# One layer of a hybrid S5 and attention trunk: second keys behind the output projection, memory scaled at eviction, and the first up pair by seven block products

## The chip, the core and the metric

The kernel runs on one core of one Trainium2 chip, as one launch that computes a whole layer in float32. TensorE (PE) multiplies, VectorE (DVE), ScalarE (ACT) and GpSimd (POOL) work on tiles, SyncE (SP) issues most of the loads, POOL most of the stores. The metric is the device time of an execution in microseconds: the median of 3 runs was 1415.62 us (1415.24 to 1419.94).

## The reference

The batch is 1, with 1024 rows of 1024 channels, 256 memory rows, 4 cross-attention heads of 256 and a feed-forward width of 2816.

```python
def memory_cross_attention(h, mem_n, wq, wkv, wo):
    q = (h @ wq).reshape(bsz, seq, XA_HEADS, XA_HEAD_DIM)
    kv = mem_n @ wkv
    k = kv[..., :D_MODEL].reshape(bsz, m, XA_HEADS, XA_HEAD_DIM)
    v = kv[..., D_MODEL:].reshape(bsz, m, XA_HEADS, XA_HEAD_DIM)
    s = jnp.einsum('bqhd,bmhd->bhqm', q, k).astype(jnp.float32) / math.sqrt(XA_HEAD_DIM)
    p = jax.nn.softmax(s, axis=-1)
    o = jnp.einsum('bhqm,bmhd->bqhd', p.astype(v.dtype), v).reshape(bsz, seq, D_MODEL)
    return o @ wo

def swiglu(h, w_gate, w_up, w_down):
    return (jax.nn.silu(h @ w_gate) * (h @ w_up)) @ w_down

def reference(...):
    mem_n = rms_norm(mem, mem_g)
    h = rms_norm(x, mix_pre_g)
    proj = h @ w_in
    ...
    y_ssm = s5_mixer(...)
    y_fox = forgetting_attention(q, k, v, f_logit).reshape(bsz, seq, FOX_WIDTH)
    y_mix = jnp.concatenate([rms_norm(y_ssm, ssm_out_g), rms_norm(y_fox, fox_out_g)], axis=-1)
    x = x + rms_norm(y_mix @ w_out, mix_post_g)
    h = rms_norm(x, xa_pre_g)
    x = x + rms_norm(memory_cross_attention(h, mem_n, xa_wq, xa_wkv, xa_wo), xa_post_g)
    h = rms_norm(x, ffn_pre_g)
    x = x + rms_norm(swiglu(h, w_gate, w_up, w_down), ffn_post_g)
```

## The kernel before

Products in float32 are made of three matmuls: both operands are split into a high part, made by ACT (L113), and a low part, made by DVE as the difference (L115, or L117 with a gain), and `mm3` (L122 to L124) adds high by high, high by low and low by high. In the traces a split thus shows as an ACTIVATE at L113 followed by a TENSOR_TENSOR at L115 on the same tile. Weights are loaded by SP into `raw` (two buffers) and split into `whl` (three buffers) by `load_w`.

The stages are these. The input projection, the S5 scan and the FoX attention take the first 490 us. The attention (L732 scores, L739 and L741 the exponentials, L760 transposes, L774 values) is a chain through all engines, so other work is woven into it as fillers: the gate of the S5 branch, its rows (L838), the load and scaling of the memory (L962 on), the 16 tiles of memory keys and values (`mem_tile`, L969) and the first half of the keys (`build_a(0)`). `mem_load` multiplies the transposed memory by the reciprocal root of each memory row, broadcast over the partitions (`rb`, made by `row_bcast`), with 8 multiplications by DVE at L965; then it splits each piece. Each memory tile is evicted from PSUM by ACT (L977) and stored to `kv_d` by POOL.

The output projection follows (490 to 540 us): per row tile n, in the order 3, 4, 5, 6, 7, 0, 1, 2, the S5 part of the sum is loaded from DRAM (L1068, named `a<-t_d` or `b<-t_d` in the profile after the view that it is read through), a row tile of x is fetched (L1071), PE multiplies, DVE evicts with the addition (L1078), ACT squares (L1080), POOL multiplies by a gain (L1082), the reciprocal root follows (L137 to L145), DVE adds to x (L1086) and POOL stores (L1090). Woven in are the first value weights: value tiles are loaded into `t`, split, and multiplied with the split output weights (`g<-whl,t`, L122 to L124).

`build_a(1)` makes the other half of the keys: for two heads it loads a key tile from `kv_d` (L1006), splits it (L1007) and multiplies it with the query weights. The tiles come from the buffers "b" and "a", which the output projection uses too.

Cross-attention runs to about 770 us. The feed-forward part works on 11 pairs of tiles of 256 hidden channels. From the second pair on a product by a pair is made by the seven block products of Strassen and Winograd's scheme (`gate_up`), with operands S1 to S4 of sums and differences of weight blocks, made by POOL at L1405 and split. The first pair uses plain products, 8 block products for the gate and 8 for the up projection (`plain_product`), each of 12 matmuls of 128x512 at L1302. hB holds the activations' blocks and their sums T1 to T4. The down projection ends the kernel, from 1198 us.

The order of instructions on each engine is set by the framework's scheduler, from priorities, from `tc.issue_after` (an instruction is put behind another) and from when buffers come free. It is fixed when the kernel is built; each engine then executes its list in that order, and one that waits holds everything behind it. Buffers are counted pools: 3 of "t2", 2 of "yt", 2 each of "a" and "b", 1 of "e".

Of the kernel before, what the change touches and what calls it, by code (L numbers as in the profile page):

```python
# [52 lines left out]
def layer(ctx: ExitStack, tc: tile.TileContext, a, out):  # L53
# [113 lines left out]
        return v[:, 0], v[:, 1]  # L167

    def row_bcast(r, n):
        rb = t2t([P, n * P]) if n == 2 else tt("d", [P, n * P])  # L170
        ps = (s_ps if n > 4 else g_ps)([P, n * P])
        for j in range(n):
            pe.transpose(ps[:, j * P:(j + 1) * P], r[:, j:j + 1].broadcast_to([P, P]), ident)
        for j in range(0, n, 4):
            cs = slice(j * P, min(j + 4, n) * P)
            act.activation(out=rb[:, cs], in_=ps[:, cs], func=AF.Copy)
        return rb
# [778 lines left out]
    def mem_load(r, out):  # L956
        rb = row_bcast(r, 2)
        yield
        mh, ml = slab([P, KT, 256]), slab([P, KT, 256])
        for k in range(0, KT, 4):  # L960
            m = raw([P, 4, 256])
            sp.dma_start(out=m, in_=a["memT"].rearrange("(k p) m -> p k m", p=P)[:, k:k + 4])  # L962
            for kk in range(4):
                with behind():
                    dve.tensor_tensor(out=m[:, kk], in0=m[:, kk], in1=rb, op=ALU.mult)  # L965
# [3 lines left out]
        out.extend((mh, ml))  # L969

    def mem_tile(i, mh, ml):
        wh, wl = load_w(a["wkv"][i], P, stage="e" if i % 3 == 2 else None)
        ps = g_ps([P, 256])
        for k in range(KT):
            mm3(ps, wh[:, k], wl[:, k], mh[:, k], ml[:, k], k == 0, k == KT - 1)
        o = t2t([P, 256])
        act.activation(out=o, in_=ps, func=AF.Copy)  # L977
        stB.dma_start(out=kv_d[i], in_=o)


# [14 lines left out]
        yield from build_a(0)  # L995

    Ah, Al = {}, {}

    def build_a(c):
        for t in range(2):  # L1000
            Ah[c, t], Al[c, t] = slab([P, 4, 512]), slab([P, 4, 512])
        for h in range(2):
            hd = 2 * c + h
            kh = tt(("ea", "ba")[c][h], [P, 2, 2, 256], F32R)
            kr = kh[:, 1].bitcast(F32)
            sp.dma_start(out=kr, in_=kv_d[2 * hd:2 * hd + 2].rearrange("d p m -> p d m"))  # L1006
# [56 lines left out]
    for n, j in enumerate((3, 4, 5, 6, 7, 0, 1, 2)):  # L1063
# [4 lines left out]
                sp.dma_start(out=t[64 * i:64 * i + 64], in_=t1_d.rearrange("j (k s) d -> s k j d", s=16)[2 * j + i])  # L1068
        xt = tt("ec"[n % 4 > 0])
        with tc.issue_after(wo_read.ins):  # L1070
            sp.dma_start(out=xt, in_=a["x"][ts, :])  # L1071
        ss4, ss, r = sm(4, "ss4"), sm(1, "ss"), sm(1, "r")
        for h in range(2):
            hs = slice(h * 512, h * 512 + 512)
# [257 lines left out]
    def ev():  # L1332
        return evp.tile([P, 512], F32, name="ev", tag="ev")

    def plain_product(m, f, t):
        ps = (g_ps if t else x_ps)([P, 512])
        for n, name in enumerate((("11", "21"), ("12", "22"))[t]):
            product(ps, plain[m, f][n], name, n == 0)
        if m == 0:
            hid[f, t] = ev()  # L1340
            with tc.issue_after(tail[0].ins):
                act.activation(out=hid[f, t], in_=ps, func=AF.Silu)
        else:
            finish_hid(0, f, t, ps)

    def finish_hid(i, f, t, u):
        h = hid[f, t]
# [45 lines left out]
        split(o[:, 0], o[:, 1], src)  # L1393
        return o[:, 0], o[:, 1]

    def operands(i, m):

        rw = slab([P, 2, KT, P], F32)
        for f in range(2):
            sp.dma_start(out=rw[:, f].rearrange("p k f -> p (k f)"), in_=a[GU[m]][2 * i + f])  # L1400
        a11, a12, a21, a22 = rw[:, 0, 0:4], rw[:, 0, 4:8], rw[:, 1, 0:4], rw[:, 1, 4:8]
        s2, s3, s4 = (ssp.tile([P, 4, P], F32, name="ss", tag="ss") for _ in range(3))
        s1 = a21
        def sub(o, x, y, fn=ALU.subtract):
            made[0] = pool.tensor_tensor(out=o, in0=x, in1=y, op=fn)  # L1405
        o = {"11": op(a11)}
# [6 lines left out]
        o["12"] = op(a12)  # L1413
        o["S2"] = op(s2)
        o["22"] = op(a22)
        o["S1"] = op(s1)
        return o

    def gate_up(i, m, w, q):
        q.p1(w["11"])  # L1420
        p1 = q.keep(1)
        product(q.bank(4), w["S4"], "22", True)
        product(q.bank(3), w["S3"], "T3", True)
        p7 = q.keep(3)
        q.p2(w["12"])
# [3 lines left out]
        product(q.bank(2), w["S1"], "T1", False)  # L1429
        c21 = q.add(3, u2, False)  # L1430
# [3 lines left out]
        c = {(0, 0): q.b[1], (0, 1): c12, (1, 0): c21, (1, 1): p7}  # L1434
# [9 lines left out]
    plain[1, 1] = []  # L1444
    for n in range(2):
        w = ev()
        sp.dma_start(out=w, in_=a["w_up"][1][:, n * 512:n * 512 + 512])
        plain[1, 1].append(op(w.rearrange("p (k f) -> p k f", f=P)))
# [11 lines left out]
    hload("T1")  # L1460
    for n, (i, m) in enumerate(seq):
        if n + 1 < len(seq):
            ws[seq[n + 1]] = operands(*seq[n + 1])
# [173 lines left out]
```

## Time and profile before

| | |
|---|---|
| median of 3 runs | 1415.62 us (1415.24 to 1419.94) |
| the profiled execution | 1418.36 us, span 1416.6 us |
| mean granted clock of PE | 0.99 |
| longest wait of PE | 11.1 us, at 539.5 us |
| PE busy, 290 to 380 us | 90.00 of 90 us |
| DVE busy, 290 to 380 us | 54.73 of 90 us |
| ACT busy, 290 to 380 us | 51.19 of 90 us |

A line of a group reads: line of the kernel, engine, operation, tile written and tiles read, shape, count; then busy time and mean length, and the idle time of the engine just before them with what ended it. A line of a timeline begins with the start and the length in us. In a wait, "A <- B" means that A waited and B released it.

### The profile page before, as it was taken

Reading aid. Unit: us, or ns where it says so; the run is one execution under the profiler, and the core shown is the slowest. Engines: PE = TensorE matmul, PEld = TensorE weight load, DVE = VectorE, ACT = ScalarE, POOL = GpSimd, SP = SyncE. Lnnn points to the kernel's source line nnn. Section 1 sums busy time; section 2 is a strip of 40 time slices with the busy share of each in tenths; the row PEclk is TensorE's granted clock in tenths of the full one; section 3 lists DMA queues with packets and bytes.
Section 4 is the critical chain, followed back from the end, with each engine's and each line's share of the span. In section 5 each row is a group of like instructions: output and inputs, shape, how many; then the busy total and the mean of one; then the engine's idle time right before and its main releaser. Section 6 shows DMA issues by size and latency. Waiting matters only on the chain.

```text
span 1416.6 us, 20283 instructions
## 1 busy us (share of the span) xinstructions
PE 1378.9 (97%) x7353; PEld 1161.8 (82%) x7353; DVE 951.5 (67%) x1719; ACT 652.0 (46%) x1289; POOL 381.9 (27%) x430
## 2 busy tenths in 40 slices
PE   9999999999999996999999999999999999999997
PEld 7889888789888775888888788888888888888886
DVE  7959954857567675545457677777766676555566
ACT  7373345766566545534334532333333334544441
POOL 0011110011111152002021467676666661000021
PEclk9999999999999998999999999999999999999999
DMA  6435765367662764024557255554444446965544
GB/s 216 143 108 160 209 223 134 90 168 219 194 179 90 221 215 129 30 75 140 172 179 265 98 186 187 185 186 147 151 157 156 169 151 234 348 204 194 179 164 163
DMA packets 104629, 241.55 MB, mean 171 GB/s; under 512 B 11528, under 2 KB 40200, under 8 KB 104336
## 3 DMA queue, kind: packets, MB, share of 16 engines
q1 hardware_dynamic: 86000, 178.33, 40.0%
q0 software_dynamic: 18528, 61.91, 12.3%
q8 instruction: 58, 0.95, 0.3%
q14 instruction: 43, 0.35, 0.1%
HBM read 171.52 MB, written 79.43 MB: 177 GB/s over the span
## 4 chain that ended last, share of the span: by engine, by line
PE 59%; DVE 0%; ACT 0%; issue 0%; DVEq 0%; ACTq 0%
PE x L1302 17%; PE g L1302 13%; PE x L1565 7%; PE g L1565 7%; PE g L124 2%; PE g L122 2%; PE g L123 2%; PE x L123 2%; PE x L124 2%; PE x L122 2%; PE g L1098 1%; PE g L1209 1%; DVE whl L115 0%; ACT whl L113 0%; DVE x L1545 0%
## 5 line engine op out<-in xcount | busy, mean ns | idle before, releaser
L1302 PE MATMUL x<-slab,op 128*128 128x512 f32 x984 | 233.3, 389 | 0.5 <-DVE op L115 0.5
L1302 PEld LDWEIGHTS x<-slab,op 128*128 128x128 f32 x984 | 184.6, 188 | 39.3 <-DVE op L115 1.0
L1302 PE MATMUL g<-slab,op 128*128 128x512 f32 x744 | 178.7, 389 | 0.0
L115 DVE TENSOR_TENSOR slab<-slab 128x1024 fp32r<-128x1024 f32 (+2 forms) x96 | 115.3, 1208 | 85.9 <-ACT slab L113 83.9
L1302 PEld LDWEIGHTS g<-slab,op 128*128 128x128 f32 x744 | 139.7, 188 | 29.0
L122 PE MATMUL g<-slab,whl 128*128 128x512 f32 (+1 forms) x416 | 151.5, 364 | 0.8 <-ACT slab L487 0.4
L113 ACT ACTIVATE slab<-slab 128x1024 fp32r<-128x1024 f32 (+2 forms) x96 | 99.1, 1037 | 108.4 <-DMA slab<-hs_d 79.2
L124 PE MATMUL g<-slab,whl 128*128 128x512 f32 (+1 forms) x416 | 148.7, 358 | 0.0
L123 PE MATMUL g<-slab,whl 128*128 128x512 f32 (+1 forms) x416 | 148.4, 357 | 0.0
L1565 PE MATMUL g<-slab 128*128 128x512 f32 x462 | 126.6, 389 | 0.0
L1565 PE MATMUL x<-slab 128*128 128x512 f32 x462 | 126.6, 389 | 0.0
L1565 PEld LDWEIGHTS x<-slab 128*128 128x128 f32 x462 | 86.7, 188 | 18.0
L1565 PEld LDWEIGHTS g<-slab 128*128 128x128 f32 x462 | 86.7, 188 | 18.0
L115 DVE TENSOR_TENSOR op<-slab,op 128x512 fp32r<-128x512 f32 x80 | 83.5, 1054 | 11.6 <-ACT op L113 11.3
L122 PEld LDWEIGHTS g<-slab,whl 128*128 128x128 f32 x416 | 78.6, 189 | 12.0 <-ACT whl L113 0.6
L122 PE MATMUL g<-whl,slab 128*128 128x256 f32 (+2 forms) x288 | 86.8, 310 | 1.6 <-ACT yt L320 0.7
L124 PEld LDWEIGHTS g<-slab,whl 128*128 128x128 f32 x416 | 78.4, 189 | 11.6 <-DVE whl L115 0.2
L1378 POOL TENSOR_TENSOR wt<-wt 128x256 f32<-128x256 f32 x88 | 81.7, 929 | 21.8 <-DMA wt<-in_w_down 18.4
L123 PEld LDWEIGHTS g<-slab,whl 128*128 128x128 f32 x416 | 78.6, 189 | 10.7
L113 ACT ACTIVATE op<-slab 128x512 fp32r<-128x512 f32 x80 | 50.0, 628 | 80.1 <-PE x L1302 38.2
L123 PE MATMUL g<-whl,slab 128*128 128x256 f32 (+2 forms) x288 | 86.1, 299 | 0.0
L124 PE MATMUL g<-whl,slab 128*128 128x256 f32 (+2 forms) x288 | 85.9, 299 | 0.0
(395 smaller groups left out, 2877.2 us busy)
## 6 DMA issues: line engine op xcount, KB each, us to landing
hs_d<-ev POOLq DMA_DIRECT2D x77, 256.0 KB, 2.6
slab<-hs_d SPq DMA_DIRECT2D x35, 512.0 KB, 3.9
wt<-in_w_down SPq DMA_DIRECT2D x44, 256.0 KB, 3.3
wt_d<-wt POOLq DMA_DIRECT2D x22, 512.0 KB, 4.8
slab<-in_w_gate SPq DMA_DIRECT2D x20, 512.0 KB, 4.7
slab<-in_w_up SPq DMA_DIRECT2D x20, 512.0 KB, 4.6
slab<-wt_d SPq DMA_DIRECT2D x20, 512.0 KB, 4.6
wd_d<-in_w_down SPq DMA_DIRECT2D x33, 256.0 KB, 4.9
```

The costliest lines, as they stand in the source:

```text
L113: first = act.activation(out=hi, in_=src, func=AF.Copy, scale=1.0 if mul is None else mul)
L115: (lo_eng or dve).tensor_tensor(out=lo, in0=src, in1=hi.bitcast(F32), op=ALU.subtract)
L122: pe.matmul(ps, lh, rh, start=first, stop=False)
L123: pe.matmul(ps, lh, rl, start=False, stop=False)
L124: pe.matmul(ps, ll, rh, start=False, stop=last)
L1098: pe.transpose(tp[:, k], src[:, (k0 + k) * P:(k0 + k + 1) * P], ident)
L1209: turned = pe.transpose(tp[:, k], h3[:, (4 * n + k) * P:(4 * n + k + 1) * P], ident)
L1302: pe.matmul(ps, x[:, k], y[:, k], start=first and k + n == 0, stop=k == 3 and n == 2, skip_group_check=not first)
L1378: pool.tensor_tensor(out=o, in0=x, in1=y, op=ALU.subtract)
L1565: pe.matmul(banks[n][j], xo[:, u, js], wo[:, v], start=ends[0] and k == 0, stop=ends[1] and k == 2, skip_group_check=onto is not None)
```

## The change

Memory: `rb` takes a buffer of "yt" instead of "t2" and stays until the last memory tile. The 8 multiplications of the loaded memory fall away; each of the 16 memory tiles is multiplied by `rb` when it is evicted, by DVE instead of ACT. The product is the same, since the factor belongs to a column of the result.

Second keys: their tiles use the buffers "e" and "b"; their loads are put behind the last x fetch of the output projection, and their splits behind the exponential of its last reciprocal root.

Feed-forward: for the first pair the up projection is made by seven block products instead of eight plain ones. The first two, "11" and "21", use the weights that are split already; the S operands are made by DVE instead of POOL. The gate stays plain. The loads of single up weights fall away, the weights of the pair are loaded once in one slab; the operands of the next gate and T1 are loaded in another order.

```diff
     def row_bcast(r, n):
-        rb = t2t([P, n * P]) if n == 2 else tt("d", [P, n * P])
+        rb = tt("yt", [P, n * P]) if n == 2 else tt("d", [P, n * P])
...
                 with behind():
-                    dve.tensor_tensor(out=m[:, kk], in0=m[:, kk], in1=rb, op=ALU.mult)
                     split(mh[:, k + kk], ml[:, k + kk], m[:, kk], g_mem[:, k + kk:k + kk + 1])
...
-    def mem_tile(i, mh, ml):
+    def mem_tile(i, mh, ml, rb):
...
-        act.activation(out=o, in_=ps, func=AF.Copy)
+        dve.tensor_tensor(out=o, in0=ps, in1=rb, op=ALU.mult)
...
     def build_a(c):
...
-            kh = tt(("ea", "ba")[c][h], [P, 2, 2, 256], F32R)
+            kh = tt(("ea", "eb")[c][h], [P, 2, 2, 256], F32R)
             kr = kh[:, 1].bitcast(F32)
-            sp.dma_start(out=kr, in_=kv_d[2 * hd:2 * hd + 2].rearrange("d p m -> p d m"))
-            split(kh[:, 0], kh[:, 1], kr)
+            with tc.issue_after(x_read[0].ins) if c else ExitStack():
+                sp.dma_start(out=kr, in_=kv_d[2 * hd:2 * hd + 2].rearrange("d p m -> p d m"))
+            with tc.issue_after(x_read[1].ins) if c else ExitStack():
+                split(kh[:, 0], kh[:, 1], kr)
...
-            sp.dma_start(out=xt, in_=a["x"][ts, :])
+            x_read[0] = sp.dma_start(out=xt, in_=a["x"][ts, :])
...
-        rsqrt_mean(r, ss, D)
+        x_read[1] = rsqrt_mean(r, ss, D)[0]
...
-    def operands(i, m):
+    def operands(i, m, engine=None):
...
+            if engine:
+                engine.tensor_tensor(out=o, in0=x, in1=y, op=fn)
+            else:
+                made[0] = pool.tensor_tensor(out=o, in0=x, in1=y, op=fn)
+        o = {"11": op(a11)} if i else {}
...
-    for t in range(2):
-        for m in range(2):
-            for f in range(2):
-                plain_product(m, f, t)
-        if t == 0:
-            ws[1, 0] = operands(1, 0)
-        wd_sums(t)
-    hid_sums(0)
+    first = Products(0, 1)
+    for f in range(2):
+        plain_product(f, 0)
+    product(first.bank(1), plain[1, 0][0], "11", True)
+    second = x_ps([P, 512])
+    product(second, plain[1, 0][1], "21", True)
+    w = operands(0, 1, dve)
+    for f in range(2):
+        plain_product(f, 1)
     hslab("T1")
     hload("T1")
+    ws[1, 0] = operands(1, 0)
+    wd_sums(0)
+    with tc.issue_after(tail[0].ins):
+        p1 = first.keep(1)
+    c11 = ev()
+    dve.tensor_tensor(out=c11, in0=second, in1=p1, op=ALU.add)
+    product(first.bank(3), w["S3"], "T3", True)
+    p7 = first.keep(3)
+    product(first.bank(4), w["S4"], "22", True)
+    product(first.bank(2), w["S2"], "T2", True)
+    u2 = first.add(2, p1)
+    product(first.bank(3), w["22"], "T4", False)
+    product(first.bank(2), w["S1"], "T1", False)
+    sums(0, 1, first, p1, p7, u2, c11)
+    wd_sums(1)
```

Three places of the fixed order, before and now. In the new kernel the line numbers behind L976 are one or two higher (L1080 before is L1082 now).

The first is the order on DVE where the memory is scaled, during the attention: `raw` is the loaded memory, L739 and L742 belong to the attention. Before:

```order
L742 RECIPROCAL nlr<-nlr 128x1
L965 TENSOR_TENSOR raw<-raw,t_2767 128x256 x3
L685 SCALAR_TENSOR_TENSOR t_2712<-t_2711,t_2712 128x512
L743 TENSOR_SCALAR c<-c,nlr 128x640
L965 TENSOR_TENSOR raw<-raw,t_2767 128x256 x5
L739 ISA c,nlr<-s,b 128x768
```

Now:

```order
L742 RECIPROCAL nlr<-nlr 128x1
L685 SCALAR_TENSOR_TENSOR t_2712<-t_2711,t_2712 128x512
L743 TENSOR_SCALAR c<-c,nlr 128x640
L739 ISA c,nlr<-s,b 128x768
L739 ISA nlr 128x1
```

The multiplications no longer stand ahead of the attention's L739.

The second is the order on ACT at the end of the output projection: `a` and `b` are row tiles in L1080 and second keys in L113, `t_5907` is a value tile. Before:

```order
L1080 ACTIVATE yt,ss_5712<-b 128x256 x2
L113 ACTIVATE a<-a 128x512
L137 ACTIVATE rsy<-ss,epsc 128x1
L138 ACTIVATE rsy<-rsy 128x1
L1080 ACTIVATE yt,ss_5774<-a 128x256 x2
L113 ACTIVATE whl<-raw 128x1024
L1080 ACTIVATE yt,ss_5774<-a 128x256 x2
L113 ACTIVATE b<-b 128x512
L137 ACTIVATE rsy<-ss,epsc 128x1
L138 ACTIVATE rsy<-rsy 128x1
L113 ACTIVATE slab<-g 128x512
L1080 ACTIVATE yt,ss_5842<-b 128x256 x2
```

Now, from the last squares on (`t_5898` is the value tile):

```order
L1082 ACTIVATE yt,ss_5834<-b 128x256 x2
L113 ACTIVATE t_5898<-t_5899 128x512
L113 ACTIVATE whl<-raw 128x1024
L113 ACTIVATE slab<-g 128x512
L1082 ACTIVATE yt,ss_5834<-b 128x256 x2
L113 ACTIVATE slab<-g 128x512
L137 ACTIVATE rsy<-ss,epsc 128x1
L113 ACTIVATE slab<-g 128x512
L138 ACTIVATE rsy<-rsy 128x1
L113 ACTIVATE e<-e 128x512
L113 ACTIVATE b<-b 128x512
L113 ACTIVATE slab<-g 128x512
```

Both splits of second keys stand behind the value tile's split and behind the last L138.

The third is the order on DVE at the start of the feed-forward part: `ss` is an S operand, `op` a split operand, the slab of 128x2048 is T1. Before:

```order
L1348 TENSOR_TENSOR ev<-x,ev 128x512
L1348 TENSOR_TENSOR ev<-g,ev 128x512
L115 TENSOR_TENSOR op<-ev,op 128x512
L1363 TENSOR_TENSOR ev<-ev 128x512
L115 TENSOR_TENSOR op<-ev,op 128x512
L115 TENSOR_TENSOR op<-slab,op 128x512
```

Now:

```order
L1405 TENSOR_TENSOR ss<-slab 128x512
L1405 TENSOR_TENSOR slab<-slab 128x512
L1405 TENSOR_TENSOR ss<-slab 128x512
L1405 TENSOR_TENSOR ss<-slab,ss 128x512
L115 TENSOR_TENSOR slab<-slab 128x2048
L115 TENSOR_TENSOR op<-ss,op 128x512 x3
```

The four sums and differences come first, then T1's low half, and only then the low halves of the S operands.

More of the change, by code (lines that the diff above doesn't have):

```diff
@@ L968, in mem_load @@
                     yield
-        out.extend((mh, ml))
-    def mem_tile(i, mh, ml):
+        out.extend((mh, ml, rb))
+    def mem_tile(i, mh, ml, rb):
         wh, wl = load_w(a["wkv"][i], P, stage="e" if i % 3 == 2 else None)
@@ L997, in layer @@
     Ah, Al = {}, {}
+    x_read = [None, None]
     def build_a(c):
@@ L1333, in ev, with plain_product @@
         return evp.tile([P, 512], F32, name="ev", tag="ev")
-    def plain_product(m, f, t):
+    def plain_product(f, t):
         ps = (g_ps if t else x_ps)([P, 512])
         for n, name in enumerate((("11", "21"), ("12", "22"))[t]):
[L1338 to L1344, printed above, removed]
+            product(ps, plain[0, f][n], name, n == 0)
+        hid[f, t] = ev()
+        with tc.issue_after(tail[0].ins):
+            act.activation(out=hid[f, t], in_=ps, func=AF.Silu)
     def finish_hid(i, f, t, u):
@@ L1404, in sub @@
         def sub(o, x, y, fn=ALU.subtract):
-            made[0] = pool.tensor_tensor(out=o, in0=x, in1=y, op=fn)
-        o = {"11": op(a11)}
+            if engine:
[3 more added lines that the diff above has]
+        o = {"11": op(a11)} if i else {}
         sub(s3, a11, a21)
@@ L1412, in operands @@
         o["S4"] = op(s4)
-        o["12"] = op(a12)
+        if i:
+            o["12"] = op(a12)
         o["S2"] = op(s2)
@@ L1429, in gate_up, with sums @@
         product(q.bank(2), w["S1"], "T1", False)
+        sums(i, m, q, p1, p7, u2, q.b[1])
+    def sums(i, m, q, p1, p7, u2, c11):
         c21 = q.add(3, u2, False)
@@ L1433, in gate_up @@
         c12 = q.add(4, u4, False)
-        c = {(0, 0): q.b[1], (0, 1): c12, (1, 0): c21, (1, 1): p7}
+        c = {(0, 0): c11, (0, 1): c12, (1, 0): c21, (1, 1): p7}
         if m == 0:
@@ L1442, in gate_up @@
             hid_sums(i)
[L1444 to L1448, printed above, removed]
     seq = [(i, m) for i in range(1, NPAIR) for m in range(2)]
     ws = {}
-    for t in range(2):
-        for m in range(2):
-            for f in range(2):
-                plain_product(m, f, t)
-        if t == 0:
-            ws[1, 0] = operands(1, 0)
-        wd_sums(t)
-    hid_sums(0)
+    first = Products(0, 1)
[7 more added lines that the diff above has]
+        plain_product(f, 1)
     hslab("T1")
     hload("T1")
+    ws[1, 0] = operands(1, 0)
+    wd_sums(0)
+    with tc.issue_after(tail[0].ins):
+        p1 = first.keep(1)
[10 more added lines that the diff above has]
+    wd_sums(1)
     for n, (i, m) in enumerate(seq):
```

## The prediction

> **What bounds the kernel now.** I read the page first, then the list of what TensorE (PE) waited for (engine, waiting line, releaser, us in total, times, longest).
>
> ```profile
> span 1416.6 us, 20283 instructions
> PE 1378.9 (97%) x7353; PEld 1161.8 (82%) x7353; DVE 951.5 (67%) x1719; ACT 652.0 (46%) x1289; POOL 381.9 (27%) x430
> ...
> PE g L122 <- ACT t L113: 11.1, 1, 11.1
> PE s L732 <- DVE nlr L739: 3.5, 3, 2.0
> PE g L760 <- ACT t L838: 2.8, 2, 2.5
> ```
>
> PE is idle for 1416.6 − 1378.9 = 37.7 us in all. So time is won only by fewer matmuls, by matmuls at a higher clock, or at one of a few waits; the largest is one single wait of 11.1 us. The timelines of PE, SyncE's queue (SPq), ACT and DVE around it (start, duration, engine, line, operation; at the end a DMA group with its us to landing):
>
> ```profile
> 539.12 0.39 PE L124 MATMUL g<-whl,t 128*128 128x512 f32 x1
> 550.58 0.79 PE L122 MATMUL g<-whl,t 128*128 128x512 f32 x1 [11.07 <-ACT t L113]
> ...
> 561.35 0.38 PE L124 MATMUL g<-b,whl 128*128 128x256 f32 x1 [0.83 <-DVE whl L115]
> ...
> 522.99 1.25 SPq L1068 DMA_DIRECT2D b<-t_d  x2
> 525.78 0.33 SPq L1071 DMA_DIRECT2D c<-in_x  x1
> 528.14 0.38 SPq L1006 DMA_DIRECT2D a<-kv_d  x1
> ...
> 540.56 0.63 ACT L113 ACTIVATE a<-a 128x512 fp32r<-128x512 f32 x1 [10.19 <-DMA a<-kv_d]
> ...
> 546.99 0.63 ACT L113 ACTIVATE b<-b 128x512 fp32r<-128x512 f32 x1 [1.05 <-DMA b<-kv_d]
> ...
> 549.91 0.61 ACT L113 ACTIVATE t<-t 128x512 fp32r<-128x512 f32 x1
> ...
> 541.23 0.69 DVE L115 TENSOR_TENSOR a<-a 128x512 fp32r<-128x512 f32 x1 [10.47 <-ACT a L113]
> 541.84 0.74 DVE L1078 SCALAR_TENSOR_TENSOR a<-x,r_f,a 128x512 f32<-128x512 f32 x1
> ...
> 548.33 0.74 DVE L1078 SCALAR_TENSOR_TENSOR b<-x,r_f,b 128x512 f32<-128x512 f32 x1
> ...
> t<-kv_d SPq DMA_DIRECT2D x1, 256.0 KB, 7.5
> ```
>
> PE stops at 539.51, though its value tile `t` needs no late data. ACT stands in its queue at the split of second keys (`a<-a`), whose load was issued at 528.14 and lands at 540.5. Behind that split stand the squares and reciprocal roots of the last three row tiles, and only behind those the split of `t` at 549.91. DVE stands at the low half of the same keys for 10.47 us. When PE comes back, its clock is halved (windows: PE busy, DVE, ACT, POOL, PEclk, DMA share, GB/s):
>
> ```profile
> 539.50:551.00 11.50, 0.43 (x2) 0.42 (x2) 8.46 (x15) 7.18 (x22) 4.20 (x3) 0.61 0.30 98
> 551.00:556.00 5.00, 5.00 (x13) 3.85 (x13) 3.88 (x7) 2.18 (x7) 3.60 (x2) 0.53 0.20 38
> ```
>
> **Part B, second keys.** The loads go behind the last x fetch, and the splits behind the last reciprocal root. No instruction is added. What waits now at the old place? DVE goes straight on from row tile 5 to 6 and 7, which need their t1 tiles (the profile calls them `a<-t_d`, `b<-t_d`) in SBUF. No view prints when the last, `b<-t_d`, landed: issued up to 524.24, it lands after 531.7 if it takes the 7.5 us of the quickest load of this stretch, and hardly after 540.5, when the later issued `a<-kv_d` had arrived. The trace's semaphore events put it near 538.5; that value I take. (The Trainium skill, "DMA: Bandwidth & Descriptors", Queues, rings and completion order, says that descriptors of one row are consumed in ring order but completion is not first in, first out; so 540.5 is by that rule no strict bound.) From 538.5: DVE's L1078 0.74, then ACT's split of `t`, 0.61, with squares and small operations between, and PE restarts at about 540.7 instead of 550.58. The next binding operation was DVE's low half of a query weight (`whl`), which released PE at 561.35, 11.4 us after the split of `t` began. The same chain from 540.1 ends at about 551.6. From there PE was saturated before and should be after. Gain 561.35 − 551.65 = 9.7 us; I take 9.3 for a little half clock. Low end 6: landing at 540.5 costs 2.0, and the new place of the key splits up to 1.5 more, since ACT now has `e<-e` and `b<-b` directly ahead of that `whl`. High end 12: part of those 11.4 us was DVE and ACT waiting for a PE at half clock.
>
> **Part A, memory scaling.** Timelines, and the group of DVE multiplications that disappears:
>
> ```profile
> L965 DVE TENSOR_TENSOR raw<-raw,t 128x256 f32<-128x256 f32 x8 | 2.8, 417 | 0.0
> ...
> 274.92 0.50 PE L732 MATMUL s<-slab,a 128*128 128x512 f32 x1 [1.99 <-DVE nlr L739]
> ...
> 276.97 1.86 PE L239 MATMUL g<-ones,d 128*128 128x1 f32 x8 [0.60 <-DVE d L691]
> ...
> 281.08 0.41 PE L124 MATMUL g<-whl,slab 128*128 128x256 f32 x1
> 281.29 0.41 PE L122 MATMUL g<-whl,slab 128*128 128x256 f32 x1
> ...
> 285.94 0.40 PE L760 MATMUL g<-ident,c 128*128 128x128 f32 x1 [2.48 <-ACT t L838]
> ...
> 292.39 0.28 PE L122 MATMUL g<-whl,slab 128*128 128x256 f32 x1
> 292.51 0.28 PE L123 MATMUL g<-whl,slab 128*128 128x256 f32 x1
> ...
> 283.44 1.06 ACT L113 ACTIVATE whl<-raw 128x1024 fp32r<-128x1024 f32 x1 [2.60 <-DMA raw<-in_wkv]
> ```
>
> The eight multiplications (2.8 us) stand directly ahead of the L739 for which PE waits 1.99 us; without them that wait and the 0.60 at L239 go. The wait of 2.48 for L838 is ACT's queue again: L838 stood behind `whl<-raw`, which waited for a weight load; in the new order L838 stands ahead of it. That is 5.07 us. But the load does not come sooner, so PE, earlier by that much, meets it at the first memory tile: 1.6 to 2 us, worked out from the landing at 283.4 and the 1.06 and 1.2 us of the two split halves; I take 1.8. Between 276 and 290 PE ran 24 such matmuls at 0.21 us instead of 0.12 (the pairs of rows): 24 × 0.09 = 2.2 us, half of which I count as won. Net 5.07 − 1.8 + 1.1 = 4.4, say 4.5; ends 0.5 (all of the waits come back as the load wait) and 7.
>
> Against this stand 16 evictions, which move from ACT to DVE (290 to 380; window, then groups with mean ns):
>
> ```profile
> 290.00:380.00 90.00, 90.00 (x751) 80.92 (x748) 54.73 (x116) 51.19 (x107) 12.71 (x21) 1.00 0.71 207
> ...
> L115 DVE TENSOR_TENSOR whl<-raw,whl 128x1024 fp32r<-128x1024 f32 x11 | 13.4, 1223 | 7.1 <-ACT whl L113 7.0
> L117 DVE SCALAR_TENSOR_TENSOR slab<-g,gains,slab 128x256 fp32r<-128x256 f32 x6 | 2.9, 479 | 0.7 <-ACT slab L113 0.7
> ...
> L977 ACT ACTIVATE t<-g 128x256 f32<-128x256 f32 x16 | 5.8, 365 | 0.0
> ```
>
> A 128x256 eviction by DVE costs about the 479 ns of L117: 16 × 0.48 = 7.7 us more on a DVE that is busy 54.73 of 90, and 5.8 less on ACT. PE is busy 90.00 of 90 here and has other matmul groups between; I cost it at nothing. That cover gone, it is rival 2.
>
> **Part C, up projection of the first pair.** From the chain (start, us, pieces) and the timelines:
>
> ```profile
> 773.67 12.47 PE x L1302 x55
> 786.14 0.87 PE g L1209 x8
> ...
> 807.71 0.55 issue
> ...
> 795.72 3.89 POOL L1405 TENSOR_TENSOR ss<-slab 128x512 f32<-128x512 f32 x1 [5.47 <-DVE t L1236]
> ...
> 797.77 0.68 DVE L115 TENSOR_TENSOR slab<-t,slab 128x512 fp32r<-128x512 f32 x1
> ...
> 807.64 0.69 DVE L1348 TENSOR_TENSOR ev<-g,ev 128x512 f32<-128x512 f32 x1 [8.59 <-PE g L1302]
> ...
> 816.35 2.28 DVE L115 TENSOR_TENSOR slab<-slab 128x2048 fp32r<-128x2048 f32 x1
> ```
>
> One matmul takes 12.47 / 55 = 0.227 us; 8 block products of 12 become 7, so 12 × 0.227 = 2.7 us less, and the 0.55 at 807.71 goes with the operation it waited for. New: gates and the two products from plain weights end at 773.67 + 120 × 0.227 + 0.87 = 801.8. DVE must have S3 ready by then. It is free at 798.45, makes four subtractions (0.68 each, to 801.2), then the 2.28 of T1, which stands ahead in its queue, then S3's low half: 804.1. Some matmuls on high halves come first, so PE waits 0.9 to 1.5; DVE's 8.59 us of idle time cover the rest. Net 2.7 + 0.55 − 1.1 = 2.2; ends −1 and 3.3 (no wait).
>
> **The sum.** 9.3 + 4.5 + 2.2 = 16.0. The profiled execution took 1418.36 us (span 1416.6 and 1.8 around it), 2.7 above the median 1415.62: 1402.4 on its basis, about 1400 on the median's.
>
> **The rivals.**
> 1. The keys' wait only moves. The new loads of kv_d wait for their buffers and for x, take 12.3 us like the old one, and ACT stands at `e<-e` ahead of the query weight. For it: the DMA share stays high to 540. Against: `b<-kv_d`, issued last, held ACT for 1.05 us only. B falls to 3 or 4: 1400 + 6 = 1406. Chance 0.15.
> 2. DVE's evictions hold PE up, on the slow side. If each memory tile finds one `whl` half (1.22) and one operation on 128x512 (0.7) ahead of its eviction, and PE has no free bank, PE waits 16 × 1.92 = 30.7: 1400 + 31 = 1431. It decides from a mean wait of 1 us per tile, where the whole gain of 16 is used up. Against: PE's 90.00 of 90 with six DVE evictions there already. Chance 0.05.
> 3. The up operands come late: T1's data or the late gate weights hold DVE or ACT, PE waits up to 4 us more than I say: 1404. For it: T1 in front, and a first POOL subtraction of 3.89 us shows how long an operand can take. Chance 0.15.
> 4. The clock. After a gap of 1.99 us at 272.9 the granted clock here fell (0.21 us a matmul at 281), so in B's stretch several short waits may halve it again: two windows at half speed, some 3 us, 1403. Chance 0.15. The Trainium skill, "TensorE: Matmul & The Clock Gate", HAM oscillation, gives gaps over about 3.4 us as the danger; by that rule none of these waits would do it and B would be 9.7. The trace does not agree, with its 1.99.
>
> The forecast with all three parts near their values has 0.45; something else giving back most of it 0.05.
>
> **Numbers.** 1400. Part bounds together reach from 1415.6 − 22 = 1393 to 1415.6 − 5.5 = 1410, and rivals 1, 3 and 4 lie inside; I widen the low end to 1391. About 0.5% (7.1 us) is what a measurement of this kernel tells from no change: faster means under 1408.5. All but rival 2, the unnamed case and the tails of rival 1 lie there: faster 0.84, same 0.11, slower 0.05.
>
> **What would show it.** Right in B: no PE wait near 11 us at 540, `e<-e` split without a long wait for kv_d, granted clock above 0.9 between 540 and 556. Right in A: no L965, PE's waits for L739 and L838 gone near 275 and 286, a short wait for the weights of the first memory tile; PE still 90 of 90 while the tiles run. Right in C: the matmul group of the product line 12 fewer, one wait of about a microsecond near the start of the S3 product. It would be wrong if a wait of 5 us or more stands at the second keys, or if PE waits at the evictions.

## The result

The changed kernel took 1407.38 us in the median of 5 executions (1401.89 to 1409.09), before 1415.62 (5 executions, 1413.39 to 1419.94): ratio 0.9932, 95% interval 0.9908 to 0.9956. Two later comparisons, on other occasions, gave 0.9919 (0.9899 to 0.9939) and 0.9936 (0.9916 to 0.9957). The ratios here and below are those on record, taken over the executions of a comparison; they are not the quotients of the medians. So it is faster by 8 to 11 us, not by 16. The profiled execution happened to be the fastest of the five, 1401.89 us with a span of 1400.1, 16.5 less than the one before; read alone it would confirm the forecast to half a microsecond, and that would be an accident. The page and PE's waits in it:

```profile
span 1400.1 us, 20288 instructions
PE 1370.7 (98%) x7341; PEld 1153.5 (82%) x7341; DVE 976.5 (70%) x1740; ACT 651.2 (47%) x1278; POOL 378.2 (27%) x430
...
PE g L124 <- DVE t L115: 1.8, 2, 1.4
PE g L122 <- ACT t L113: 1.6, 1, 1.6
PE g L1304 <- DVE ev L1325: 1.6, 2, 1.4
```

The wait of 11.1 us has become one of 1.6 at the same matmul. A new wait stands in the list, for an addition by DVE at L1325. A second profile of the same kernel (1405.8 us) was taken in the experiments, and a third (1407.3 us); PE's waits in the third:

```profile
PE g L1304 <- DVE ev L1325: 4.2, 1, 4.2
PE g L774 <- ACT yt L787: 2.2, 1, 2.2
PE g L124 <- DVE t L115: 1.8, 2, 1.4
```

Here the new wait is 4.2 us. Since the kernel's stages follow one another on a full PE, each can be timed by the starts of PE's matmuls. The line views give them; these rows (first and last start behind the durations) are of the kernel before:

```profile
L732 PE MATMUL s<-slab,a x96: 220/394/504, 230.2 to 458.7; 128*128 128x512 f32 x48, 128*128 128x128 f32 x16, 128*128 128x256 f32 x16, 128*128 128x384 f32 x16
...
L760 PE MATMUL g<-ident,c x288: 270/273/475, 234.5 to 476.8; 128*128 128x128 f32 x144
...
L1302 PE MATMUL x<-slab,whl x72: 389/389/476, 773.5 to 790.5; 128*128 128x512 f32 x72
...
L1565 PE MATMUL g<-slab x462: 389/389/389, 1194.5 to 1401.6; 128*128 128x512 f32 x154
```

and these of the changed kernel's third profile:

```profile
L732 PE MATMUL s<-slab,a x96: 220/396/500, 229.4 to 453.1; 128*128 128x512 f32 x48, 128*128 128x128 f32 x16, 128*128 128x256 f32 x16, 128*128 128x384 f32 x16
...
L760 PE MATMUL g<-ident,c x288: 270/273/330, 233.7 to 471.2; 128*128 128x128 f32 x144
...
L1304 PE MATMUL x<-slab,whl x72: 387/389/473, 757.7 to 774.7; 128*128 128x512 f32 x72
...
L1582 PE MATMUL g<-slab x462: 389/389/389, 1183.3 to 1390.5; 128*128 128x512 f32 x154
```

From the first L732 to the last L760 is the attention (part A), from there to the first feed-forward matmul the output projection, the second keys and cross-attention (part B), and from there to the first matmul of the down projection the products by pairs (part C). All profiles of this study, in us:

| profile | attention | output, keys, cross | feed-forward products |
|---|---|---|---|
| before | 246.6 | 296.7 | 420.95 |
| changed, first / second / third | 240.9 / 242.0 / 241.8 | 287.2 / 285.5 / 286.5 | 420.94 / 425.64 / 425.65 |
| memory alone | 246.9 | 296.7 | 420.91 |
| keys alone | 244.5 | 285.9 | 420.91 |
| seven products alone | 245.9 | 296.4 | 420.95 |
| memory and keys | 244.5 | 285.8 | 420.91 |
| first keys later | 242.9 | 289.0 | 420.95 |
| gate sums by DVE (twice) | 245.0 / 245.1 | 285.9 / 289.0 | 418.78 / 418.75 |
| down sums later | 244.8 | 287.1 | 419.23 |
| first keys early | 242.0 | 287.0 | 418.75 |

The down projection takes 214.65 us from its first to its last matmul in every one of them. What lies ahead of the attention ends between 228.6 and 231.2.

### The profile page after: what moved, and what is told of

Read it like the earlier page. It is cut to its first block, busy times and chain, and to the rows that moved or that the text cites. A ratio compares the mean times of both kernels' runs of the same rounds, so it can differ in the third digit from the quotient of the medians.

```text
span 1400.1 us, 20288 instructions
## 1 busy us (share of the span) xinstructions
PE 1370.7 (98%) x7341; PEld 1153.5 (82%) x7341; DVE 976.5 (70%) x1740; ACT 651.2 (47%) x1278; POOL 378.2 (27%) x430
## 4 chain that ended last, share of the span: by engine, by line
PE 58%; DVE 2%; issue 1%; ACT 1%; DVEq 0%
PE x L1304 16%; PE g L1304 12%; PE x L1582 7%; PE g L1582 7%; PE g L124 2%; PE g L122 2%; PE g L123 2%; PE x L123 2%; PE x L124 2%; PE x L122 2%; PE g L1100 1%; DVE op L115 1%; PE g L1211 0%; DVE slab L115 0%; DVE whl L115 0%
## 5 line engine op out<-in xcount | busy, mean ns | idle before, releaser
L1304 PE MATMUL g<-slab,op 128*128 128x512 f32 x756 | 182.2, 390 | 1.8 <-DVE ev L1325 1.6
L113 ACT ACTIVATE slab<-slab 128x1024 fp32r<-128x1024 f32 (+2 forms) x96 | 99.1, 1038 | 101.7 <-DMA slab<-hs_d 76.9
L115 DVE TENSOR_TENSOR op<-slab,op 128x512 fp32r<-128x512 f32 x82 | 96.9, 1191 | 11.4 <-ACT op L113 11.0
L122 PE MATMUL g<-whl,slab 128*128 128x256 f32 (+2 forms) x288 | 85.3, 305 | 3.4 <-ACT slab L765 1.3
L113 ACT ACTIVATE op<-slab 128x512 fp32r<-128x512 f32 x82 | 51.2, 627 | 78.7 <-PE x L1304 39.9
L113 ACT ACTIVATE op<-ss 128x512 fp32r<-128x512 f32 x63 | 39.6, 630 | 102.8 <-PE g L1304 54.3
L124 PE MATMUL g<-whl,slab 128*128 128x256 f32 (+2 forms) x288 | 84.8, 295 | 0.0
```

The costliest lines, as they stand in the source:

```text
L113: first = act.activation(out=hi, in_=src, func=AF.Copy, scale=1.0 if mul is None else mul)
L115: (lo_eng or dve).tensor_tensor(out=lo, in0=src, in1=hi.bitcast(F32), op=ALU.subtract)
L122: pe.matmul(ps, lh, rh, start=first, stop=False)
L124: pe.matmul(ps, ll, rh, start=False, stop=last)
L1304: pe.matmul(ps, x[:, k], y[:, k], start=first and k + n == 0, stop=k == 3 and n == 2, skip_group_check=not first)
```

## The experiments

**Each part alone.** Three kernels, each with one part of the change.

The memory alone:

```diff
-        rb = t2t([P, n * P]) if n == 2 else tt("d", [P, n * P])
+        rb = tt("yt", [P, n * P]) if n == 2 else tt("d", [P, n * P])
...
-                    dve.tensor_tensor(out=m[:, kk], in0=m[:, kk], in1=rb, op=ALU.mult)
...
-        act.activation(out=o, in_=ps, func=AF.Copy)
+        dve.tensor_tensor(out=o, in0=ps, in1=rb, op=ALU.mult)
```

> The kernel before with the memory scaling at eviction alone. Theory (each part gains by itself what the two profiles show between the same places: attention 5.7 us): 5 to 7 us faster than before, about 1409 to 1411, PE's wait of 1.99 at L739 and of 2.48 at L838 gone, PE still busy 88 to 90 of 90 us between 290 and 380. Rival (the gain of the attention comes from the other parts' reordering or from a clock that happened to be full): within 2 us of before, about 1415. Rival (evictions by DVE cost PE waits): slower than before.

Measured: 1417.08 us against 1417.42, ratio 0.9991 (0.9978 to 1.0004). This can't be told from no change; the rival "within 2 us of before" holds for the time, though the waits at L739 and L838 are gone as the theory said. PE's waits in its profile:

```profile
PE g L122 <- ACT t L113: 11.3, 1, 11.3
PE g L774 <- ACT yt L787: 2.6, 1, 2.6
...
PE g L122 <- ACT slab L765: 1.3, 1, 1.3
```

and its stretches at the two places (PE busy first, PEclk third from the end):

```profile
276.00:284.00 8.00, 6.66 (x35) 6.43 (x35) 6.59 (x18) 7.02 (x18) 0.72 (x1) 0.57 0.51 152
...
373.00:380.00 7.00, 5.39 (x35) 3.34 (x36) 3.67 (x8) 4.35 (x11) 1.75 (x2) 0.76 0.10 29
```

Two waits came in place of the ones removed, 1.3 at 276 and 2.6 at 372, and behind both the clock is halved. The three profiles of the changed kernel have the same two waits, of 1.34 and of 1.2 to 2.4, without a half clock behind them, and their attention is 4.9 to 6.0 us shorter. But 1.6 us of this lies elsewhere: this profile has a third stretch of half clock, at the start of the attention, behind two waits of PE of 0.9 and 0.6 us for L739 that all thirteen profiles have. PE's stretch there (busy, clock, DMA share, GB/s) in this kernel and in one without a half clock at that place, the last kernel of this section:

```profile
232.00:236.00 4.00, 3.86 (x12) 0.57 0.92 311
...
232.00:236.00 4.00, 3.30 (x17) 1.00 1.05 318
```

From the first L732 to the products at L239 behind the wait for L691, PE takes 45.9 us in this profile and 44.3 in those of the changed kernel. The stretch lies ahead of everything that the edit moves: up to 262 us PE, DVE and ACT of the changed kernel execute the same order as before. It also stands in the profiles of first keys later, of both gate sums by DVE and of down sums later (0.58 to 0.88 from 232 to 236), and in no other. So what the part is worth in a profile is decided by where the clock falls, and part of that has nothing to do with the part.

The keys alone:

```diff
-            kh = tt(("ea", "ba")[c][h], [P, 2, 2, 256], F32R)
+            kh = tt(("ea", "eb")[c][h], [P, 2, 2, 256], F32R)
...
+            with tc.issue_after(x_read[0].ins) if c else ExitStack():
+                sp.dma_start(out=kr, in_=kv_d[2 * hd:2 * hd + 2].rearrange("d p m -> p d m"))
+            with tc.issue_after(x_read[1].ins) if c else ExitStack():
+                split(kh[:, 0], kh[:, 1], kr)
```

> The kernel before with the second keys behind the output projection alone. Theory: the 11 us wait of PE near 540 goes, 9 to 10 us faster, about 1406, with the clock full from 540 to 556. Rival (the wait is gone but short waits keep the clock halved): 5 to 7 us faster, about 1409, and PEclk near 0.5 in a stretch between 530 and 560. Rival (the wait only moves to the keys): a wait of 4 us or more at the key products, 1411 or later.

Measured: 1406.28 us, ratio 0.9918 (0.9898 to 0.9937). This part alone is as fast as the whole change. Its stretches at the place where PE stood before:

```profile
530.00:540.00 10.00, 8.45 (x37) 6.68 (x36) 7.38 (x13) 6.04 (x18) 4.23 (x3) 1.00 0.85 280
540.00:551.00 11.00, 9.41 (x52) 7.57 (x51) 10.59 (x20) 8.35 (x21) 2.35 (x2) 1.00 0.47 138
551.00:556.00 5.00, 4.95 (x35) 4.17 (x34) 4.08 (x10) 4.64 (x9) 0.00 (x0) 1.00 0.19 73
```

PE is busy 9.41 of 11 us where it was 0.43 of 11.5, the clock is full where it was 0.61 and 0.53, and the stage takes 285.9 instead of 296.7 us. The rivals "half clock" and "the wait moves to the keys" fall here.

The seven products alone:

```diff
-    for t in range(2):
-        for m in range(2):
-            for f in range(2):
-                plain_product(m, f, t)
...
+    w = operands(0, 1, dve)
...
+    sums(0, 1, first, p1, p7, u2, c11)
```

> The kernel before with the seven block products of the first pair alone. Theory (DVE backlog eats the saving: DVE is full from 776 to 832 in the changed kernel, its operations stretched from 0.68 to 1.2 to 1.8 us while POOL makes the sums of the next gate): within 1 us of before, about 1415, with one or more PE waits for DVE's L1325 of 1 us or more behind the first pair. Rival (the saving of 12 matmuls stands, 2.2 us as predicted): about 1413.5.

Measured: 1419.94 us, ratio 1.0018 (1.0001 to 1.0035). Not a gain of 2.2 but, if anything, a loss. In its profile the stage takes exactly what it took before, 420.95, with 12 matmuls less: a wait of 1.37 at L1323 (L1325 in the full change) and four of 0.2 to 0.3 take back 2.25 of the 3.27 us that the matmuls and the old wait of 0.55 had cost; the last microsecond shows in no single wait. The profiled execution, 1417.06 us, is one of the faster of its twelve, so where the others lose is not shown.

**The changed kernel again, and a third time** (unaltered).

> The changed kernel once more, unaltered. Theory (most executions halve PE's clock somewhere for some 14 us, which the profiled execution of 1401.9 did not): median 1406 to 1408, mean clock of most executions 0.993 to 0.996, and time and clock go together, at about 3 to 4 us per 0.003 of the mean clock. Rival (the differences between executions come from DMA, not the clock): times that differ by 4 us or more at the same mean clock.

Measured: 1407.0 us, ratio 0.9919 (0.9899 to 0.9939), mean clocks 0.994 to 0.997. Time and clock go together only roughly: the six executions have 1404.41 at 0.997 and 1408.46 at 0.994, but also 1408.78 at 0.995 and 1405.77 at 0.996.

> The changed kernel, unaltered, a third time. Theory: 0.9920 to 0.9930 of before, and a feed-forward part of 420.9 to 425.7 us, by how long POOL's sums and DVE's splits collide. Rival (the wait of 4.16 us in the second profile was a single event): 420.9 as in the first profile.

Measured: 1406.79 us (1403.81 to 1414.78), ratio 0.9936 (0.9916 to 0.9957); four executions at a clock of 0.996 lie between 1403.8 and 1407.3, a fifth at 1410.2. These 6.4 us at one mean clock are what the rival of the comparison before named as its sign, so the clock alone does not explain the spread. In the second and the third profile the feed-forward products take 425.6 us, so the long wait is no single event; two of the three profiles have it. Timeline of DVE and of POOL in the third profile:

```profile
797.76 0.68 DVE L115 TENSOR_TENSOR op<-ss,op 128x512 fp32r<-128x512 f32 x1
798.36 6.73 DVE L115 TENSOR_TENSOR op<-slab,op 128x512 fp32r<-128x512 f32 x1
805.01 0.68 DVE L115 TENSOR_TENSOR op<-ss,op 128x512 fp32r<-128x512 f32 x1
805.62 0.68 DVE L1325 TENSOR_TENSOR ev<-g,ev 128x512 f32<-128x512 f32 x1
...
798.74 0.76 POOL L1377 TENSOR_TENSOR wt<-wt 128x256 f32<-128x256 f32 x1
799.42 1.31 POOL L1407 TENSOR_TENSOR ss<-slab 128x512 f32<-128x512 f32 x1
800.68 0.74 POOL L1377 TENSOR_TENSOR wt<-wt 128x256 f32<-128x256 f32 x1
801.37 1.28 POOL L1407 TENSOR_TENSOR slab<-slab 128x512 f32<-128x512 f32 x1
802.61 0.72 POOL L1377 TENSOR_TENSOR wt<-wt 128x256 f32<-128x256 f32 x1
803.29 1.25 POOL L1407 TENSOR_TENSOR ss<-slab 128x512 f32<-128x512 f32 x1
```

One DVE subtraction of 0.68 us takes 6.73. It begins just ahead of six POOL operations that follow each other without a pause, and ends half a microsecond after the last of them. In the first profile the same two queues met differently, and DVE and POOL took turns:

```profile
799.31 1.77 DVE L115 TENSOR_TENSOR op<-ss,op 128x512 fp32r<-128x512 f32 x1
801.01 0.68 DVE L1325 TENSOR_TENSOR ev<-g,ev 128x512 f32<-128x512 f32 x1
801.61 3.52 DVE L115 TENSOR_TENSOR op<-slab,op 128x512 fp32r<-128x512 f32 x3
...
801.64 1.79 POOL L1407 TENSOR_TENSOR slab<-slab 128x512 f32<-128x512 f32 x1
```

Each DVE operation with two inputs in SBUF then takes 1.2 to 1.8, and each POOL operation is longer too; further on in that profile, at 808, one DVE operation takes 3.35 us beside two POOL operations in a row. L1325, which reads PSUM and one tile in SBUF, keeps its 0.68 throughout; the stretched ones read two tiles in SBUF. (The Trainium skill, "SBUF — State Buffer", SBUF: two separate sides, says that VectorE with two SBUF inputs and GpSimd lock one shared pair of ports for a whole instruction, and that the other waits. The traces agree in which operations are stretched; that DVE may be held over six POOL instructions is more than the sentence says.)

**The seven products left out.** Memory and keys, with the plain first pair of before.

> The changed kernel with the plain first pair of before: memory scaling and second keys alone. Theory (the seven block products cost rather than gain, 0 to 7 us by execution, and the memory scaling gains nothing): 1 to 4 us faster than the changed kernel, about 1404, so near the kernel with the keys alone (1406). Rival (the gains of keys and memory add up and the seven products are neutral): 1400 or below. Rival (the seven products gain their 2 us here): 1409.

Measured: 1404.82 us, ratio 0.9916 (0.9902 to 0.9930). Its median lies 2 us below the changed kernel's medians of 1406.8 to 1407.4, as the theory has it, but these are from other comparisons and the intervals overlap. Together with 420.9 against 420.9 to 425.6 us in the profiles it says that the seven products, as made, gain nothing and sometimes lose.

**POOL's work taken away from there.**

```diff
-    ws[1, 0] = operands(1, 0)
-    wd_sums(0)
+    ws[1, 0] = operands(1, 0, dve)
...
-    wd_sums(1)
...
         wd_sums(n + 2)
+        if n in (10, 12):
+            wd_sums((n - 10) // 2)
```

> The changed kernel, with the four sums of the next gate's weights made by DVE instead of POOL, and POOL's first two pieces of the down weights moved to the middle of the loop: POOL does hardly any arithmetic between 783 and 810 us. DVE gets four more operations of 0.69 us. Theory (DVE's operations are stretched while POOL works): the operations of 1.2 to 6.75 us shrink to 0.7 or so, PE's wait of up to 4 us for L1325 goes, 2 to 4 us faster than the changed kernel, about 1404. Rival (DVE has simply too many operations here, whatever POOL does): 2.8 us more of backlog, a longer wait and the same time or more.

Measured: 1404.0 us, ratio 0.9904 (0.9891 to 0.9916). DVE has four operations more and PE waits less: the wait at L1325 is gone and the stage takes 418.78 us, 2.17 less than before, the size that the prediction gave (2.2).

> The kernel of the sums by DVE once more, beside the changed kernel on the same chip. Theory: the feed-forward part takes 418.8 us against 420.9 or more, and the median lies 2 to 4 us below the changed kernel's. Rival (what it gained lies within the spread of executions): within 1 us of the changed kernel.

Measured: 1402.65 us, ratio 0.9893 (0.9877 to 0.9910), against the changed kernel's 1406.79 and 0.9936 (0.9916 to 0.9957) in the same comparison; these intervals do not overlap. POOL does no arithmetic in it between 778 and 801, and its DVE timeline shows the subtractions of the third order above short again:

```profile
790.81 2.29 DVE L115 TENSOR_TENSOR slab<-slab 128x2048 fp32r<-128x2048 f32 x1 [0.34 <-ACT slab L113]
793.02 1.89 DVE L115 TENSOR_TENSOR op<-ss,op 128x512 fp32r<-128x512 f32 x3
794.83 1.29 DVE L115 TENSOR_TENSOR op<-slab,op 128x512 fp32r<-128x512 f32 x2
```

In the changed kernel's first profile the last two took 2.99 and 3.48 us.

With only the down sums moved, and the gate's sums still made by POOL:

```diff
-    wd_sums(0)
...
-    wd_sums(1)
...
         wd_sums(n + 2)
+        if n in (10, 12):
+            wd_sums((n - 10) // 2)
```

> The changed kernel with POOL's first two pieces of the down weights (L1377) moved to the middle of the loop, nothing else: POOL still makes the sums of the next gate's weights. Theory (stretching by POOL): the wait for L1325 near 800 is at most 1 us, since POOL is free between its two groups of sums, 1 to 3 us faster than the changed kernel. Rival (too many operations on DVE): no change, and the wait of 1.4 to 4.2 us stays at 800 to 824.

Measured: 1405.15 us, ratio 0.9918 (0.9906 to 0.9930). The wait at L1325 is gone and the stage takes 419.23 us. The rival "too many operations on DVE" falls: DVE's work is the same, and only what POOL does beside it differs. The long operation itself is not gone; it stands at another place, beside six POOL operations again:

```profile
812.03 6.17 DVE L115 TENSOR_TENSOR op<-slab,op 128x512 fp32r<-128x512 f32 x1
```

No wait of PE over 0.3 us is left in this stretch (790 to 835), so what counts is whether PE needs DVE at that moment. As a time the 1 to 3 us are not separated from the changed kernel.

**The second wait of the attention.** In the third profile of the changed kernel ACT stands at the split of the first keys, ahead of the eviction that PE needs:

```profile
371.06 0.63 ACT L113 ACTIVATE e<-e 128x512 fp32r<-128x512 f32 x1 [4.81 <-DMA e<-kv_d]
371.60 0.37 ACT L787 ACTIVATE yt<-g 128x256 f32<-128x256 f32 x1
```

It is the situation of the second keys once more, on a smaller scale. First, in the kernel of memory and keys, the split was put behind a later eviction:

```diff
+    late = [None]
...
-                act.activation(out=sq, in_=yp, func=AF.Square)
+                late[0] = act.activation(out=sq, in_=yp, func=AF.Square)
...
-            with tc.issue_after(x_read[1].ins) if c else ExitStack():
+            with tc.issue_after((x_read[1] if c else late[0]).ins):
```

> As the kernel of memory scaling and second keys alone, with one edit: the split of the first keys stands on ACT behind a later L787 (eviction of attention values) instead of ahead of the one that PE waits for near 370 us. Theory (the memory scaling gains 5 us at 273 to 284 and gives 2.5 us and the clock window behind it back at this place): PE's wait for yt near 370 goes, no half clock at 376 to 380, 2 to 4 us faster than without this edit, about 1401. Rival (the wait only moves to the next step of the attention, or the missing first keys leave PE without filler work): the same or slower, with a wait of 2 us or more between 370 and 460.

Measured: 1404.77 us, ratio 0.9912 (0.9898 to 0.9926), the same as memory and keys without it (0.9916). PE's waits in its profile:

```profile
PE g L122 <- ACT t L113: 2.4, 1, 2.4
PE g L122 <- ACT a L113: 2.3, 1, 2.3
```

The wait near 370 is gone, and the second of these, at 457.6, is new: PE waits for the split of the next head's keys. The attention is 1.6 us shorter than without the edit (242.9 against 244.5), though it has the half clock at 232 to 236 that the other lacks; the stage behind it is 3.2 us longer (289.0 against 285.8), with 2.4 us of waiting for `t` (the first of these rows) where the other has 0.9. For the time, the rival "the wait only moves" holds. That the longer wait for `t` follows from the edit is not shown: the same stage took 285.9 and 289.0 in two profiles of one kernel.

Then the load was made possible earlier instead, by keeping its buffer free (on top of the kernel with the gate's sums by DVE):

```diff
-            wh, wl = load_w(a["w_out_s"][cc], 256, stage="e" if cc == 2 else None)
+            wh, wl = load_w(a["w_out_s"][cc], 256, stage=None)
...
-        wh, wl = load_w(a["wkv"][i], P, stage="e" if i % 3 == 2 else None)
+        wh, wl = load_w(a["wkv"][i], P, stage="e" if i % 3 == 2 and i < 12 else None)
```

> The kernel of the sums by DVE, with the buffer e no longer used to stage the third weight of the S5 rows and the last weight of the memory tiles, so that the first keys' load can be issued some 20 us earlier and their split does not wait on ACT for it near 370 us. Theory (PE's wait of 1.2 to 2.6 us for yt near 370 comes from that split's wait for kv_d): the wait goes, the attention is 2 to 4 us shorter than with the sums by DVE alone, about 1401 to 1402 where that kernel has 1404. Rival (weights that are no longer staged come late instead): PE waits for whl between 300 and 400, the same time or more.

Measured: 1400.57 us (1399.92 to 1402.96), ratio 0.9884 (0.9869 to 0.9899). The split now waits 1.35 us, at 341.8, where nothing stands behind it that PE needs at once:

```profile
341.82 0.63 ACT L113 ACTIVATE e<-e 128x512 fp32r<-128x512 f32 x1 [1.35 <-DMA e<-kv_d]
```

No wait of PE over half a microsecond is left between 277 and 458 us. The attention takes 242.0 us although the clock is halved at 276 to 284, 3 us less than in the two profiles with the sums by DVE alone, which have that half clock and the wait (245.0 and 245.1). Only half of this is the edit's: the other two have the half clock at 232 to 236 as well, 1.6 us, ahead of the place that the edit clears. This is the fastest kernel of the study, 17 us faster than before and 6 us faster than the changed kernel in the same comparison, with intervals apart (0.9899 against 0.9916). Against the kernel that it differs from by this one edit, 1402.65, it is 2 us faster, and these intervals overlap (up to 0.9899, from 0.9877), so as a time the edit is not separated.

## Why the prediction was right, and where it was not

The time lies within the range (1391 to 1410) and the direction is as forecast; the likeliest value, 1400, is 7 us too low by the first comparison. By its own steps:

- **Part B, 9.3 us**: measured 296.7 − 286.4 = 10.3 in the mean of the three profiles of the changed kernel, and a ratio of 0.9918 for the part alone. Right in mechanism and size. The term that was taken from the trace's semaphores, the landing of the last t1 tile, is what DVE waits for now that the splits of the keys no longer stand there; the same wait in the second profile and in the first:

```profile
531.20 0.75 DVE L1080 SCALAR_TENSOR_TENSOR b<-x,r_f,b 128x512 f32<-128x512 f32 x1 [1.76 <-DMA b<-t_d]
...
532.72 0.75 DVE L1080 SCALAR_TENSOR_TENSOR b<-x,r_f,b 128x512 f32<-128x512 f32 x1 [2.54 <-PE x L124]
```

  The first profile names PE, but the product that this addition reads, the fifteenth of sixteen, had ended at 529.27. The sixteenth ended at 532.67, by chance beside the landing of the tile (532.60 by the semaphore events). The nine other profiles with this part name the load, with 1.6 to 2.5 us. So the restart still hangs on that load: the stage's two longest times, 289.0, go with PE's two longest waits for the split of `t`, 2.4 and 2.8 us, where the others have 0.9 to 1.6. The chain from the split of `t` to PE's saturation, 11.4 us before, is 10.6 now (534.32 to 544.94 in the first profile).
- **Part A, 4.5 us**: the step that failed is "net 5.07 − 1.8 + 1.1". Of the 5.07 of waits 4.7 went (0.35 stays at L239). The wait of 1.34 that takes their place is near the 1.8 of the sum, but by luck: the sum had PE meet the late load of the first memory tile's weights, and PE waits for ACT's L765 instead (275.88 to 276.46 in the first profile), while the split of those weights waits 0.66 us for its load at 280.87 and holds PE nowhere. A second wait of 1.2 to 2.6, behind the first keys' split, was not in the sum. And the 1.1 for a faster clock came in the three profiles of the changed kernel and in none of the seven others with this part, although PE, DVE and ACT execute the same order from 229 to 330 us in all ten. Attentions without this part took 246.6, 244.5 and 245.9, mean 245.7; the eight profiles with it whose attention is otherwise as in the change (the three of the change, 246.9, 244.5, 245.0, 245.1 and 244.8) have a mean of 243.9. So some 1.8 us; without the 1.6 us that the half clock at 232 costs four of the eight it would be some 2.6. The time shows neither: the part alone has 0.9991, and memory and keys have 0.9916 where the keys alone have 0.9918. Costing the 16 evictions at nothing was right: 6.8 us by DVE, and no wait of PE for them in the first profile (PE is busy 88.81 of 90 us from 290 to 380, and the rest is the wait of 1.2 near 370):

```profile
L976 DVE TENSOR_TENSOR t<-g,yt 128x256 f32<-128x256 f32 x16 | 6.8, 423 | 8.6 <-PE g L124 5.2 <-DMA kv_d<-t 3.0
```

- **Part C, 2.2 us**: the step that failed is "DVE's 8.59 us of idle time cover the rest". The 12 matmuls went, and PE's waits near the S3 product are 0.15 and 0.27 in the first profile, less than the 0.9 to 1.5 of the sum. But the durations in the sum were those of a DVE that works beside an idle POOL. The load of the next gate's weights, which the change puts behind T1, is issued at 783.1, 26 us behind the first product of the pair, where it was issued at 772.3, 1.2 us ahead of that product. So POOL's sums fall into DVE's fullest stretch, and its operations take 1.2 to 6.7 us instead of 0.68. PE pays 1.6 to 4.2 us at L1325, and in two of three profiles a halved clock behind it. Rival 3 named late gate weights and 4 us, but as a wait for the operands, not as a slower DVE. One of its own rows held the sign: POOL's subtraction of 3.89 us at 795.72, where the shortest of its kind takes 1.28, ran beside a DVE that worked without a pause up to 799.05; it was read as the time that an operand takes. Measured 0.0 to −4.7; with POOL's sums out of this stretch 2.17.
- **The sum.** 10.3 + 1.8 − (0 to 4.7) gives 7.4 to 12.1, and the three comparisons gave 8.2, 10.4 and 10.9. The first profile had the best of both accidents, no half clock before 1390 us and the milder meeting of DVE and POOL.
- **Rival 4, the clock**, is partly true. The stretch of B kept its full clock, as in the sum, in the profiles of the change; in the second profile of the sums by DVE it fell there too, behind the wait of 2.8 us (0.73 and 0.84 from 538 to 546). In the attention a stretch of half clock costs 1.0 to 1.9 us; the changed kernel has none of them and takes 241 to 242 us, the memory alone has three and takes 246.9. The clock fell behind a wait of 0.95 to 1.34 us at 275 to 281 in all seven other profiles with part A, so gaps far shorter than the one that rival 4 quotes were enough here. What decides whether it falls was not settled: at the same wait of 1.34, in the same order of instructions, the three profiles of the changed kernel stay at full speed.

## What to carry to other kernels

When an engine waits in its queue for a load, find what stands behind the waiting instruction, and either put the wait behind what the bound engine needs or let the load begin earlier. The first worked for the second keys and gained no time for the first keys; the second took the first keys' wait away. In these traces operations of DVE with two SBUF inputs cost what their row says only while POOL rests: before work is put on DVE, look at what POOL does at the new time. When the profile names a releaser that had long been done, look at the same wait in another execution. And a change of a per cent should not be read from one profile: the stages of three profiles of one kernel differed by up to 4.7 us.

## What the runs showed of the hardware that was not expected

A 128x512 subtraction by DVE with two SBUF inputs, 0.68 us beside an idle POOL, took 6.73 us beside six POOL operations in a row (6.75 and 6.17 in two other profiles), and 1.2 to 1.8 where the two engines took turns, at the same place of the same program. Additions with one PSUM input kept 0.68 us throughout. Waits of PE of 0.95 to 1.34 us near 277 us were followed by a halved clock (0.50 to 0.53 in windows of 4 us) in seven profiles and not in three, with the same order of instructions; two waits of 0.9 and 0.6 us near 230 were followed by one in five of thirteen.
